# Every third weight subtract of the in-projection on GpSimd instead of VectorE

## The chip, the cores and the metric

The kernel runs on one core of a Trainium2 chip. The metric is the device time of one execution in microseconds; a profile of one execution, taken by the hardware profiler, comes with it. The engines are named as the profile names them: PE (TensorE, matmuls), PEld (its weight loads), DVE (VectorE), ACT (ScalarE), POOL (GpSimd) and SP (SyncE, which issues most DMAs).

## The reference

A two-layer streaming encoder on 256 tokens of width 1024, in float32. Each layer has a token mixer (retention and a convolution branch, both fed by one input projection), cross-attention into 256 memory tokens, and a gated MLP. The change touches the input projection `w_in`, 1024 x 10240 in each layer:

```python
def mixer_sublayer(u, cos, sin, w_in, ...):
    p = u @ w_in
    q, k, v, g_ret, c_in, gates = jnp.split(p, cuts, axis=-1)
    q = rotary(q, cos, sin) * (RET_QK_DIM ** -0.5)
    k = rotary(k, cos, sin)
    o = head_group_norm(chunk_retention(q, k, v), ret_gn_g)
    y_a = (jax.nn.silu(g_ret) * o) @ w_ret_out
    a, b = jnp.split(c_in, 2, axis=-1)
    c = causal_dwconv(a * jax.nn.sigmoid(b), conv_dw_w, conv_dw_b)   # 31 taps
    y_b = jax.nn.silu(layer_norm(c, conv_ln_g, conv_ln_b)) @ w_conv_out + b_conv_out
    g_a, g_b = jnp.split(jax.nn.sigmoid(gates + b_gate), 2, axis=-1)
    return (g_a * y_a + g_b * y_b) @ w_mix_out
```

## The kernel before

Every float32 matrix product is made of three products in the faster format `float32r`: each operand is split into a high half, the value rounded to that format, and a low half, what the rounding left (value minus high half). High times high, high times low and low times high are added up in PSUM.

**The weights.** All weights stream through SBUF. They are cut into chunks of 128 x 2048 (1 MB, one DMA issued by SP into one of four `raw` buffers) and each chunk into two units of 128 x 1024. `prepare` (L150) makes the halves of one unit: ScalarE copies `raw` to `whi` (L155), and VectorE subtracts, `wlo = raw - whi` (L156). There are four buffers of `whi` and four of `wlo` (`UNITS`), and `run` (L160) calls `prepare` until it is four units ahead of the steps whose matmuls have been issued. 420 units are prepared: in each layer 80 of `w_in` (78 in layer 0, whose first chunk is split elsewhere), 16 of `w_ret_out`, 16 of `w_xkv`, 8 each of four other matrices, 44 of `w_up` and 24 or 22 of the down projection.

**The in-projection** comes first in each layer: 8 chunks for the convolution branch (`in_b`, `in_a`), the first four on the not yet normalised input, then for each of four heads q and k (2 chunks), v and the gate g (4 chunks in all, through `token_step`), then 8 chunks for the merging gates. Between the matmuls of the heads stand the pieces of retention: `scores`, `attend`, whose normalisation takes a reciprocal root on GpSimd (L691, `rs`), which VectorE then multiplies by the mean (L693, `nmr`), and `gate`, where TensorE transposes the result (L703) and VectorE and ScalarE split it (L710, L711).

**The 31 taps of the convolution** are spread over the same steps as background work: most by ScalarE's product and VectorE's add (`tap`, L581 and L584), every third of half the channels by VectorE alone (`tap_alone`, L590), and 21 per layer by ScalarE into one of two buffers `moved` and an accumulating DMA issued by GpSimd (`tap_moved`, L599 and L602). In layer 0 VectorE also makes the rotary tables (L451 to L480) in the first 80 us.

**What sets the order.** The program is written step by step, and a scheduler with a model of time then sets the order of each engine's queue; each engine works through its own queue in that order and waits by semaphores. So an edit of one engine's work moves instructions of others.

Of the kernel before, what the change touches and what calls it, by code (L numbers as in the profile page):

```python
# [7 lines left out]
F32 = mybir.dt.float32  # L8
# [3 lines left out]
ALU = mybir.AluOpType  # L12
# [65 lines left out]
class Trunk:  # L78
    def __init__(self, ctx, tc, io):
        self.tc, self.nc, self.io = tc, tc.nc, io  # L80
        pool = lambda name, bufs, **kw: ctx.enter_context(tc.tile_pool(name=name, bufs=bufs, **kw))
        self.cp = pool("const", 1)
        self.wp = pool("weights", 3)
        self.bp = pool("blocks", 1)
        self.sp = pool("small", 2)
        self.pp = pool("psum", 1, space=bass.MemoryType.PSUM)
        self.steps = []
        self.uid = 0
        self.raws = {}
        self.streaming = False  # L90
        self.pin = None
        self.planned = 0
        self.background = []


    def nm(self, s):
# [53 lines left out]
    def prepare(self, src, at, kt, cols):  # L150
        nc, n = self.nc, kt * cols
        raw = self.fetch(src)[:, at:at + n]
        hi = self.wp.tile([P, 1024], F32R, name=self.nm("whi"), tag="whi", bufs=UNITS)
        lo = self.wp.tile([P, 1024], F32R, name=self.nm("wlo"), tag="wlo", bufs=UNITS)
        self.latest = nc.scalar.activation(hi[:, :n], raw, AF.Copy).ins  # L155
        nc.vector.tensor_tensor(lo[:, :n], raw, hi[:, :n].bitcast(F32), op=ALU.subtract)  # L156
        v = lambda t: t[:, :n].rearrange("p (k c) -> p k c", k=kt)
        return v(hi), v(lo)

# [1094 lines left out]
```

## Time and profile before

| | us |
|---|---|
| three runs: median (lowest to highest) | 1265.89 (1264.91 to 1268.05) |
| the profiled execution's own time | 1265.35 |
| its span, first to last instruction | 1263.5 |
| mean granted TensorE clock in it | 0.998 of full speed |
| L155 (copy to `whi`, ScalarE), 420 instructions | 439.5 |
| L156 (subtract to `wlo`, VectorE), 420 instructions | 508.0 |
| GpSimd's own work: L602 (issue of 42 DMAs), L691 (16 roots), L274 (9 roots) | 36.9, 17.0, 11.6 |

A row of a group names the line, the engine and the operation, what it writes and reads with the shape, the count, the busy time and the mean duration in ns of one; behind the second bar stands the idle time of the engine just before these instructions and what ended most of it. A row of a timeline begins with its start and its duration in us; where it ends with `x2` it is two instructions merged. A row of waits gives the total, the number of waits and the longest. Matmuls are pipelined: one begins before the one ahead of it has ended, and a busy TensorE is a TensorE that has something in its pipe.

### The profile page before, as it was taken

How to read it: one execution, taken by the hardware profiler on the slowest of the kernel's cores; microseconds unless marked ns; L12 is line 12 of the kernel's file. 1: busy time of each engine (PE TensorE's matmuls, PEld its weight loads, DVE VectorE, ACT ScalarE, POOL GpSimd, SP SyncE). 2: the span in 40 equal slices, each digit the busy share in tenths (PEclk: the TensorE clock that was granted, in tenths of full speed). 3: DMA queues.
4: the chain of work that ended last, by engine and by line, in shares of the span. 5: the costliest groups of instructions: out<-in, count | busy, mean ns of one | idle time of the engine just before them, and what ended most of it. 6: DMA issues, size and time to landing. Idle time of an engine off the chain costs nothing.

```text
span 1263.5 us, 18274 instructions
## 1 busy us (share of the span) xinstructions
PE 1251.2 (99%) x6914; PEld 1085.4 (86%) x6914; DVE 1010.9 (80%) x1540; ACT 858.8 (68%) x1428; POOL 66.8 (5%) x73
## 2 busy tenths in 40 slices
PE   9999999999999999999999999999999999999997
PEld 8988888888888898888898888888888888988886
DVE  7989988788787588886588899887887767888853
ACT  6798788867366456765458988788565565677642
POOL 0001111100000000000000111111000000000000
PEclk9999999999999999999999999999999999999999
DMA  8677787885554355554555877779754543455550
GB/s 311 213 237 218 216 234 217 244 282 179 195 172 162 113 194 199 195 192 161 205 190 186 252 210 219 228 209 278 270 179 160 195 159 142 171 212 198 177 192 34
DMA packets 40487, 252.66 MB, mean 200 GB/s; under 512 B 4688, under 2 KB 5968, under 8 KB 13520
## 3 DMA queue, kind: packets, MB, share of 16 engines
q1 hardware_dynamic: 34064, 228.96, 50.7%
q0 software_dynamic: 6048, 22.02, 9.1%
q8 instruction: 54, 0.88, 0.3%
q10 hardware_dynamic: 288, 0.52, 0.1%
q14 instruction: 33, 0.27, 0.1%
HBM read 228.42 MB, written 1.05 MB: 182 GB/s over the span
## 4 chain that ended last, share of the span: by engine, by line
PE 94%; DMA 2%; DVE 2%; ACT 1%; issue 1%; SPq 0%; POOL 0%; POOLq 0%; DVEq 0%
PE mm L239 32%; PE mm L214 28%; PE mm L212 14%; PE mm L1123 5%; PE mm L200 3%; PE mm L198 3%; PE mm L199 3%; PE mm L318 1%; PE mm L680 1%; DVE wlo L156 1%; DMA acc<-moved 1%; PE mm L926 1%; PE mm L928 1%; DMA raw<-in_mem_dram 1%; PE mm L927 1%
## 5 line engine op out<-in xcount | busy, mean ns | idle before, releaser
L155 ACT ACTIVATE whi<-raw 128x1024 fp32r<-128x1024 f32 (+1 forms) x420 | 439.5, 1053 | 297.0 <-PE mm L214 131.5
L156 DVE TENSOR_TENSOR wlo<-raw,whi 128x1024 fp32r<-128x1024 f32 (+1 forms) x420 | 508.0, 1214 | 134.2 <-ACT whi L155 120.4
L214 PE MATMUL mm<-blk,whi 128*128 128x512 f32 x1552 | 515.1, 395 | 0.0
L239 PE MATMUL mm<-whi,blk 128*128 128x512 f32 x1280 | 404.2, 392 | 0.0
L212 PE MATMUL mm<-blk,wlo 128*128 128x256 f32 x1552 | 391.5, 280 | 0.0
L214 PEld LDWEIGHTS mm<-blk,whi 128*128 128x128 f32 x1552 | 288.3, 188 | 63.2 <-DVE blk L190 0.7
L212 PEld LDWEIGHTS mm<-blk,wlo 128*128 128x128 f32 x1552 | 277.4, 189 | 5.3 <-DVE wlo L156 0.8
L239 PEld LDWEIGHTS mm<-whi,blk 128*128 128x128 f32 x1280 | 239.5, 188 | 48.7
L239 PE MATMUL mm<-wlo,blk 128*128 128x512 f32 x640 | 249.5, 391 | 0.0
L239 PEld LDWEIGHTS mm<-wlo,blk 128*128 128x128 f32 x640 | 120.3, 188 | 24.0
L581 ACT ACTIVATE prod<-blk,params 128x255 f32<-128x255 f32 (+20 forms) x224 | 94.1, 488 | 0.0
L200 PE MATMUL mm<-blk,wlo 128*128 128x256 f32 x288 | 81.4, 283 | 0.5 <-DVE wlo L156 0.5
L198 PE MATMUL mm<-blk,whi 128*128 128x256 f32 x288 | 81.8, 284 | 0.0
L199 PE MATMUL mm<-blk,whi 128*128 128x256 f32 x288 | 81.5, 283 | 0.0
L584 DVE TENSOR_TENSOR blk<-blk,prod 128x1020 f32<-128x1020 f32 (+21 forms) x56 | 65.5, 1170 | 8.2 <-ACT prod L581 7.7
L599 ACT ACTIVATE moved<-blk,params 128x227 f32<-128x227 f32 (+20 forms) x168 | 69.1, 482 | 0.0
L227 DVE TENSOR_TENSOR t<-mm,t 128x256 f32<-128x256 f32 x140 | 56.0, 415 | 2.3 <-ACT t L226 1.9
L200 PEld LDWEIGHTS mm<-blk,wlo 128*128 128x128 f32 x288 | 55.1, 191 | 0.6 <-DVE wlo L156 0.6
L198 PEld LDWEIGHTS mm<-blk,whi 128*128 128x128 f32 x288 | 55.1, 191 | 0.1
L199 PEld LDWEIGHTS mm<-blk,whi 128*128 128x128 f32 x288 | 55.1, 191 | 0.0
L602 POOL DMA_DIRECT2D acc<-moved x42 | 36.9, 878 | 342.0 <-ACT moved L599 206.5
L1123 PE MATMUL mm<-whi,blk 128*128 128x512 f32 x176 | 54.3, 389 | 0.0
(172 smaller groups left out, 1187.2 us busy)
## 6 DMA issues: line engine op xcount, KB each, us to landing
raw<-in_w_in_dram SPq DMA_DIRECT2D x79, 1024.0 KB, 4.8
raw<-in_w_up_dram SPq DMA_DIRECT2D x44, 1024.0 KB, 4.8
acc<-moved POOLq DMA_DIRECT2D x42, 512.0 KB, 5.4
raw<-in_w_ret_out_dram SPq DMA_DIRECT2D x16, 1024.0 KB, 6.6
raw<-in_w_xkv_dram SPq DMA_DIRECT2D x16, 1024.0 KB, 4.8
raw<-in_w_last_dram SPq DMA_DIRECT2D x11, 1024.0 KB, 4.8
raw<-in_w_conv_out_dram SPq DMA_DIRECT2D x8, 1024.0 KB, 4.8
raw<-in_w_mix_out_dram SPq DMA_DIRECT2D x8, 1024.0 KB, 4.8
```

The lines of the kernel that those rows point to most:

```text
L155: self.latest = nc.scalar.activation(hi[:, :n], raw, AF.Copy).ins
L156: nc.vector.tensor_tensor(lo[:, :n], raw, hi[:, :n].bitcast(F32), op=ALU.subtract)
L198: self.nc.tensor.matmul(out, wh[:, k, :], uh[:, k0 + k, :], start=a, stop=False)
L199: self.nc.tensor.matmul(out, wh[:, k, :], ul[:, k0 + k, :], start=False, stop=False)
L200: self.nc.tensor.matmul(out, wl[:, k, :], uh[:, k0 + k, :], start=False, stop=b)
L212: self.nc.tensor.matmul(ps[:, 0, :], w[1][:, k, :], u[0][:, k, :], start=False, stop=i == end)
L214: self.nc.tensor.matmul(ps, w[0][:, k, :], u.tile[:, k], start=i == 0, stop=False)
L239: mm = lambda a, b, p, q: self.nc.tensor.matmul(outs[t], a, b, start=p, stop=q)
L581: nc.scalar.activation(t[:, i, :m], X["c"][:, k, :m], AF.Copy, scale=self.par("conv_dw_w", L, k * TAPS + TAPS - 1 - s))
L584: nc.vector.tensor_tensor(cc, cc, t[:, :, :m], op=ALU.add)
L599: nc.scalar.activation(t[:, i, s:], X["c"][:, 4 + i, :N - s], AF.Copy, scale=self.par("conv_dw_w", L, (4 + i) * TAPS + TAPS - 1 - s))
L1123: mm = lambda x, y, p, e: self.nc.tensor.matmul(out, x, y[:, j, :], start=p, stop=e)
```

## The change

A counter of units is added to the class. Where a unit belongs to `w_in` and its number is a multiple of three, the same subtract is called on GpSimd in place of VectorE. Nothing else is edited; lines behind the edit are two higher.

```diff
@@ -90,7 +90,7 @@
         self.streaming = False
         self.pin = None
         self.planned = 0
-        self.background = []
+        self.background, self.count = [], 0
@@ -153,7 +153,9 @@
         hi = self.wp.tile([P, 1024], F32R, name=self.nm("whi"), tag="whi", bufs=UNITS)
         lo = self.wp.tile([P, 1024], F32R, name=self.nm("wlo"), tag="wlo", bufs=UNITS)
         self.latest = nc.scalar.activation(hi[:, :n], raw, AF.Copy).ins
-        nc.vector.tensor_tensor(lo[:, :n], raw, hi[:, :n].bitcast(F32), op=ALU.subtract)
+        self.count += 1
+        third = "w_in" in src.tensor.name and self.count % 3 == 0
+        (nc.gpsimd if third else nc.vector).tensor_tensor(lo[:, :n], raw, hi[:, :n].bitcast(F32), op=ALU.subtract)
```

The queues move at many places, since the scheduler plans anew. GpSimd's queue before, in layer 0 from the attention output of the second head to that of the third (`rs` are the reciprocal roots of the two halves of the tokens, `acc` the accumulating DMAs of the convolution):

```order
L602 DMA acc_178<-moved_27_177 128x1024
L691 TENSOR_TENSOR rs_1567<-ve_1565,mhalf 128x1
L602 DMA acc_178<-moved_26_176 128x1024
L691 TENSOR_TENSOR rs_1587<-ve_1585,mhalf 128x1
L602 DMA acc_178<-moved_27_177 128x1024
L602 DMA acc_178<-moved_26_176 128x1024
```

The same piece of GpSimd's queue in the changed kernel:

```order
L604 DMA acc_178<-moved_27_177 128x1024
L158 TENSOR_TENSOR wlo_1494<-raw_1487,whi_1493 128x1024
L693 TENSOR_TENSOR rs_1567<-ve_1565,mhalf 128x1
L604 DMA acc_178<-moved_26_176 128x1024
L158 TENSOR_TENSOR wlo_1654<-raw_1651,whi_1653 128x1024
L693 TENSOR_TENSOR rs_1587<-ve_1585,mhalf 128x1
L604 DMA acc_178<-moved_27_177 128x1024
L158 TENSOR_TENSOR wlo_1705<-raw_1698,whi_1704 128x1024
L604 DMA acc_178<-moved_26_176 128x1024
```

A subtract now stands ahead of each root and between the DMAs, and the second root waits behind `wlo_1654`. VectorE's queue before, at the same place (`nmr` needs the root of the same half; `t_242` and `t_249` are the outputs that TensorE transposes):

```order
L693 TENSOR_SCALAR nmr_1569<-mv_1563,rs_1567 128x1
L156 TENSOR_TENSOR wlo_1654<-raw_1651,whi_1653 128x1024
L658 TENSOR_TENSOR q_1536<-t_229_1537,t_230_1538 128x256
L659 TENSOR_TENSOR q_1536<-t_229_1537,t_230_1538 128x256
L689 TENSOR_SCALAR ve_1585<-mv_1583 128x1
L696 TENSOR_TENSOR t_242_1571<-t_242_1571,g_1473 128x512
L156 TENSOR_TENSOR wlo_1658<-raw_1651,whi_1657 128x1024
L693 TENSOR_SCALAR nmr_1589<-mv_1583,rs_1587 128x1
L584 TENSOR_TENSOR blk_175<-blk_175,prod_1687 128x4x245
```

And VectorE's queue there in the changed kernel:

```order
L695 TENSOR_SCALAR nmr_1569<-mv_1563,rs_1567 128x1
L660 TENSOR_TENSOR q_1536<-t_229_1537,t_230_1538 128x256
L661 TENSOR_TENSOR q_1536<-t_229_1537,t_230_1538 128x256
L691 TENSOR_SCALAR ve_1585<-mv_1583 128x1
L698 TENSOR_TENSOR t_242_1571<-t_242_1571,g_1473 128x512
L158 TENSOR_TENSOR wlo_1658<-raw_1651,whi_1657 128x1024
L695 TENSOR_SCALAR nmr_1589<-mv_1583,rs_1587 128x1
L586 TENSOR_TENSOR blk_175<-blk_175,prod_1687 128x4x245
```

Only `wlo_1654` is gone from it; what follows keeps its order. The beginning of GpSimd's streaming work in the changed kernel, where before the first root was followed by nothing until the DMAs of the convolution:

```order
L276 TENSOR_TENSOR rs_r_262<-rs_m_261,mhalf 128x2
L158 TENSOR_TENSOR wlo_152<-raw_111,whi_151 128x1024
L158 TENSOR_TENSOR wlo_301<-raw_294,whi_300 128x1024
L158 TENSOR_TENSOR wlo_472<-raw_469,whi_471 128x1024
L158 TENSOR_TENSOR wlo_551<-raw_544,whi_550 128x1024
```

Unit 3 (`wlo_152`), which VectorE subtracted right behind unit 2, now stands behind the first root, and units 6, 9 and 12 follow it. SP's queue is the same in both kernels.

## The prediction

> **What bounds the kernel now.** I read the page first: busy time, the chain that ended last, and the two groups that the change touches.
>
> ```profile
> span 1263.5 us, 18274 instructions
> PE 1251.2 (99%) x6914; PEld 1085.4 (86%) x6914; DVE 1010.9 (80%) x1540; ACT 858.8 (68%) x1428; POOL 66.8 (5%) x73
> PE 94%; DMA 2%; DVE 2%; ACT 1%; issue 1%; SPq 0%; POOL 0%; POOLq 0%; DVEq 0%
> L155 ACT ACTIVATE whi<-raw 128x1024 fp32r<-128x1024 f32 (+1 forms) x420 | 439.5, 1053 | 297.0 <-PE mm L214 131.5
> L156 DVE TENSOR_TENSOR wlo<-raw,whi 128x1024 fp32r<-128x1024 f32 (+1 forms) x420 | 508.0, 1214 | 134.2 <-ACT whi L155 120.4
> ```
>
> TensorE (PE) is busy for 99% of the span and makes 94% of the chain. GpSimd (POOL) is nearly unused. The subtract that is moved (L156) takes 1.21 us on VectorE (DVE), and VectorE has idle time in front of it, mostly waiting for ScalarE's copy. ScalarE (ACT) in its turn waits for TensorE to hand back a buffer: the weights are prepared as early as the four buffers let them be. Next I asked who TensorE ever waits for:
>
> ```profile
> PE nrm L405 <- DVE ones L391: 1.1, 1, 1.1
> PE mm L318 <- DVE blk L190: 0.7, 3, 0.3
> PE mm L680 <- ACT t L189: 0.6, 1, 0.6
> PE nrm L267 <- POOL rs_r L274: 0.5, 1, 0.5
> PE mm L200 <- DVE wlo L156: 0.5, 1, 0.5
> PE mm L318 <- ACT blk L189: 0.4, 1, 0.4
> PE nrm L259 <- DVE t L251: 0.3, 1, 0.3
> ```
>
> All waits together are 4.1 us, and one wait of 0.5 us is for a subtract. So **relieving VectorE can bring almost nothing**; the question is only whether the change makes something late enough for TensorE to notice. That is decided in the in-projection, so I took windows of it (columns: window, length, PE, PEld, DVE, ACT, POOL busy, clock, DMA share, GB/s): the early part, one period of a head in each layer, and the part of layer 1 up to its second head.
>
> ```profile
> 30.00:90.00 60.00, 60.00 (x420) 56.40 (x420) 56.53 (x82) 50.28 (x91) 1.91 (x2) 1.00 0.64 214
> 138.90:176.30 37.40, 37.40 (x186) 31.49 (x186) 33.48 (x56) 30.89 (x61) 5.69 (x6) 1.00 0.76 225
> 690.00:762.00 72.00, 71.39 (x361) 60.19 (x360) 63.77 (x95) 62.24 (x122) 7.91 (x9) 1.00 0.75 227
> 761.90:799.30 37.40, 37.40 (x187) 31.50 (x186) 33.51 (x56) 30.91 (x61) 5.69 (x6) 1.00 0.76 225
> ```
>
> The 80% of the whole is an average. Here VectorE works 33.5 of 37.4 us, and 56.5 of 60 in the early part. TensorE is at full clock and without a gap.
>
> **What is removed.** The in-projection's units, as the windows of L156 alone count them:
>
> ```profile
> 15.50:244.00 228.50, 94.18 (x78) 1.00 0.75 231
> 626.80:867.20 240.40, 96.95 (x80) 1.00 0.70 219
> ```
>
> They are 78 in layer 0 (the first chunk is prepared elsewhere) and 80 in layer 1, at places 1 to 78 and 211 to 290 of all 420; multiples of three are 26 and 26, so 52 subtracts leave VectorE. At 1.22 us that is 63 us of its busy time. Worth to TensorE: at most the 0.5 us above.
>
> **What is added.** 52 subtracts on GpSimd. No row shows one there; the nearest rows are GpSimd's own two-operand instruction on one or two elements, and VectorE's on this very tile.
>
> ```profile
> 298.38 0.70 POOL L274 TENSOR_TENSOR rs_r<-rs_m,mhalf 128x2 f32<-128x2 f32 x1 [24.30 <-DVE rs_m L273]
> 459.07 2.35 DVE L156 TENSOR_TENSOR wlo<-raw,whi 128x1024 fp32r<-128x1024 f32 x2
> 459.29 1.54 POOL L274 TENSOR_TENSOR rs_r<-rs_m,mhalf 128x2 f32<-128x2 f32 x1 [80.96 <-DVE rs_m L273]
> 138.94 1.17 DVE L584 TENSOR_TENSOR blk<-blk,prod 128x984 f32<-128x984 f32 x1
> 139.17 1.36 POOL L691 TENSOR_TENSOR rs<-ve,mhalf 128x1 f32<-128x1 f32 x1 [10.45 <-DVE ve L689]
> 176.35 1.15 DVE L584 TENSOR_TENSOR blk<-blk,prod 128x960 f32<-128x960 f32 x1
> 176.59 1.34 POOL L691 TENSOR_TENSOR rs<-ve,mhalf 128x1 f32<-128x1 f32 x1 [9.76 <-DVE ve L689]
> 213.23 1.12 DVE L584 TENSOR_TENSOR blk<-blk,prod 128x936 f32<-128x936 f32 x1
> 213.46 1.31 POOL L691 TENSOR_TENSOR rs<-ve,mhalf 128x1 f32<-128x1 f32 x1 [9.26 <-DVE ve L689]
> ```
>
> Duration: at least 1.22 us (I see no reason for GpSimd to be faster than VectorE), at most 0.70 + 2 x 1.22 = 3.14 us (its fixed cost, and the two operands read one after the other). I take 0.70 + 1.22 = **1.92 us**, nearest to both rows. [...]
>
> The same rows show the second cost. When VectorE is in a subtract or a convolution tap, that is in an instruction with two operands from SBUF, GpSimd's tiny instruction lasts 1.31 to 1.54 us in place of 0.70, and in the three pairs it shrinks by 0.02 and 0.03 us as the tap does (1.17, 1.15, 1.12): it **ends 0.42 or 0.43 us behind the tap's end** each time. GpSimd's read waits until VectorE's instruction is through. Whether VectorE waits likewise while GpSimd reads, the trace cannot show, since two elements are read in no time. [...]
>
> I take it that VectorE waits too: what makes GpSimd wait for a two-operand VectorE instruction is something that both need, and it would be as little free while GpSimd uses it. (Ends: no stop, and a stop for the whole duration.) So each moved unit takes 1.22 us off VectorE and stops it for up to 1.92 us. Not all of that stop counts: instructions with an operand from PSUM may run under it.
>
> ```profile
> L685 DVE BATCH_NORM_STATS2 bs<-mm 128x6 f32<-128x512 f32 x3 | 2.1, 692 | 0.9 <-PE mm L680 0.9
> L711 DVE SCALAR_TENSOR_TENSOR blk<-mm,params,blk 128x256 fp32r<-128x256 f32 x4 | 1.8, 476 | 0.7 <-ACT blk L710 0.7
> L227 DVE TENSOR_TENSOR t<-mm,t 128x256 f32<-128x256 f32 x4 | 1.6, 408 | 0.0
> L190 DVE TENSOR_TENSOR vlo<-mm,vhi 128x512 fp32r<-128x512 f32 x2 | 1.3, 680 | 0.0
> ```
>
> These are 6.8 of 33.5 us in the head's period, a fifth. VectorE takes its queue in order, so only those that stand at the front when GpSimd starts get through; I count half of the fifth, a tenth. The net addition to VectorE per moved unit is then 0.9 x 1.92 - 1.22 = **0.51 us** (by the ends: below nothing at 1.22, and 0.9 x 3.14 - 1.22 = 1.61 at 3.14).
>
> - Period of a head, 12 units, 4 moved: 33.48 + 2.0 = 35.5 of 37.4 us. VectorE still fits, with 1.9 us left where it had 3.9.
> - 690 to 762 us, 8 moved: 63.77 + 4.1 = 67.9 of 72. It fits.
> - 30 to 90 us, 7 moved: 56.53 + 3.6 = 60.1 of 60. **Full to the brim.**
>
> **What lies on TensorE's path.** A late VectorE costs nothing until its lateness passes what TensorE has in hand. For weights: a unit lasts TensorE 37.4 / 12 = 3.1 us and three other buffers are full, so 9.3 us less 1.05 us for the copy and 1.22 us for the subtract, some 7 us. For the attention output, the place on GpSimd's queue where a reciprocal root now stands behind a subtract:
>
> ```profile
> 143.29 0.68 DVE L696 TENSOR_TENSOR t<-t,g 128x512 f32<-128x512 f32 x1
> 148.83 0.60 PE L703 MATMUL mm<-ident,t 128*128 128x128 f32 x4
> ```
>
> The product ends at 143.97 and TensorE transposes it at 148.83: 4.9 us in hand. The new queue adds up to one subtract (1.92 us) in front of `rs_1587`; VectorE's `nmr` waits for it, and behind `nmr` the taps. That fits into 4.9 us. The accumulating DMAs on the same queue (GpSimd issues 42) start up to 1.92 us later; each frees one of two buffers, so only a delay of a whole turn would reach ScalarE. SP's queue is as before. The early part has less in hand:
>
> ```profile
> 18.28 1.61 POOL L274 TENSOR_TENSOR rs_r<-rs_m,mhalf 128x2 f32<-128x2 f32 x1 [17.83 <-DVE rs_m L273]
> 22.98 0.28 PE L200 MATMUL mm<-blk,wlo 128*128 128x256 f32 x1
> 22.40 2.83 DVE L371 SCALAR_TENSOR_TENSOR t<-h,params,nrm 128x256 f32<-128x256 f32 x7 [0.48 <-ACT rstd L361]
> 44.87 1.22 DVE L584 TENSOR_TENSOR blk<-blk,prod 128x1020 f32<-128x1020 f32 x1 [0.87 <-ACT prod L581]
> ```
>
> Unit 3 now stands behind the root that ends at 19.89: 19.89 + 1.92 = 21.81, and up to 1.22 later if a VectorE subtract is in the way, while TensorE reads it at 22.98. That costs nothing to 0.05 us. From 22.40 to the 0.87 us before 44.87 VectorE has next to no idle time, and in it makes the normalised input that TensorE needs; unit 6's stop makes that later by 1.92 - 1.22 = 0.7 us.
>
> **The sum**, against the profiled execution's own 1265.35 us (its span of 1263.5 and 1.85 around it; the median of the three runs is 0.5 higher): the normalised input 0.7; the full stretch to 90 us, 1.0 (0.1 over, and the 3.5 us of idle in it, some of which are waits for inputs that cannot be filled: from nothing to 3.5, taken near the bottom as there are buffers behind it); then 154 us of layer 0 (90 to 244) and 240 us of layer 1 (627 to 867), 394 / 37.4 = 10.5 periods at 0.3 us (ends: nothing, if all stays within the 4.9 and 7 us; 2.0, if none of the added time is filled into idle time; near the bottom for the same reason) = 3.2. Together 4.9, so **1270 us**. At a duration of 1.22 us it would be 1265.4; at 3.14 VectorE lacks 7.8 us before 90 us and 2.5 us in each period: 1265.35 + 0.7 + 7.8 + 26 = 1300.
>
> **The rivals.**
> - *VectorE is not stopped.* GpSimd's reads only wait, or slip in beside VectorE's. Then VectorE sheds 1.22 us per unit, nothing becomes late, and TensorE is where it was: 1265. For it: only one direction of the wait is seen, and the 7 and 4.9 us in hand. It decides at a stop of 1.22 / 0.9 = 1.36 us per subtract: below that VectorE gains.
> - *The subtract takes GpSimd much longer*, 2.8 to 3.14 us: VectorE's period is then 33.48 + 4 x (0.9 x 2.8 - 1.22) = 38.7 of 37.4 us and TensorE follows VectorE: 1265.35 + 10.5 x 1.3 + 7 = 1286, up to 1300. For it: nothing shows GpSimd on so many elements. Against it: nothing shows its fixed cost to grow with size.
> - *Faster*: VectorE's relief removes TensorE's waits. At most 4.1 us of waits exist, most of them in lines of the start (L405, L318, L259): 1261 to 1264.
> - *The change does not do what it says*: excluded, the built order has 52 subtracts on POOL.
>
> **How the numbers follow.** Forecast (stopped, just fitting), 1266 to 1278: 0.52. Not stopped, 1264 to 1267: 0.30. Long subtract, 1278 to 1300: 0.14. Faster: 0.04. A measurement of this kernel tells 0.3%, 3.8 us, from no change. Slower by more: the long case and 0.41 of the forecast's 0.52, so 0.55; faster 0.04; within it 0.41. The range leaves out the faster case's most and the long case's upper part: 1263.5 to 1288.
>
> **What would show it.** GpSimd's subtract at 1.9 us or more, longer where VectorE is in a tap; VectorE's two-operand instructions stretched, or idle with GpSimd as the releaser, in the in-projection alone; new TensorE waits for `wlo`, `blk` (L190) or the transposed product, first before 90 us; everything behind 867 us (layer 1) shifted and not stretched. VectorE's instructions unstretched beside a long GpSimd subtract would refute the stop; a TensorE span unchanged with stretched VectorE would mean that I mis-sized the idle time that can be filled.

## The result, and the profile after

| | before | changed |
|---|---|---|
| median (lowest to highest), us | 1265.89 (1264.91 to 1271.25) | 1281.32 (1280.53 to 1283.02) |
| runs | 5 | 5 |
| the profiled execution | 1265.35 | 1281.31 |
| its span | 1263.5 | 1279.5 |

The changed kernel takes 1.0117 times as long (95% interval 1.0097 to 1.0137), 15.4 us more by the medians. The forecast of 1270 had the direction, and the range of 1263.5 to 1288 holds the time, but the band of the forecast's own case, 1266 to 1278, does not; the loss is three times the 4.9 us of the sum.

The page of the changed kernel, its busy times, its chain and the groups that the change touches:

```profile
span 1279.5 us, 18348 instructions
PE 1255.9 (98%) x6914; PEld 1084.4 (85%) x6914; DVE 1028.9 (80%) x1488; ACT 856.9 (67%) x1428; POOL 218.1 (17%) x125
PE 76%; DVE 13%; ACT 4%; issue 3%; DMA 2%; POOL 1%; SPq 0%; POOLq 0%; DVEq 0%; ACTq 0%
L158 DVE TENSOR_TENSOR wlo<-raw,whi 128x1024 fp32r<-128x1024 f32 (+1 forms) x368 | 469.9, 1281 | 121.9 <-ACT whi L155 107.8
L158 POOL TENSOR_TENSOR wlo<-raw,whi 128x1024 fp32r<-128x1024 f32 x52 | 152.9, 2947 | 306.0 <-PE mm L214 172.4
L586 DVE TENSOR_TENSOR blk<-blk,prod 128x1020 f32<-128x1020 f32 (+21 forms) x56 | 79.0, 1410 | 16.7 <-ACT prod L583 16.4
```

52 subtracts have left VectorE, and still it is busy for 18.0 us more than before. Its remaining subtracts have gone from a mean of 1214 to 1281 ns, and the 56 taps on the last line are longer too. VectorE is now 13% of the chain, where it was 2%. The line of GpSimd's subtract by itself (least, median and greatest duration in ns, then first and last start):

```profile
L158 POOL TENSOR_TENSOR wlo<-raw,whi x52: 2375/2488/6389, 19.7 to 874.4; 128x1024 fp32r<-128x1024 f32 x52
```

Undisturbed it takes 2.4 us, twice VectorE's 1.2, but some last up to 6.4. TensorE's waits (total, number, longest), which were 4.1 us in all before, are now 13.9:

```profile
PE mm L202 <- DVE wlo L158: 3.1, 4, 1.2
PE mm L241 <- POOL wlo L158: 2.5, 3, 1.4
PE mm L241 <- DVE wlo L158: 1.5, 2, 1.1
...
PE mm L667 <- DVE k L660: 1.2, 1, 1.2
PE mm L202 <- POOL wlo L158: 0.8, 1, 0.8
PE mm L705 <- DVE nmr L695: 0.8, 1, 0.8
```

TensorE waits for low halves from both engines, and for rotated keys (`k`). These rows have grown by 9.8 us; TensorE's busy time has grown too, by 4.7 us for the same 6914 matmuls (1251.2 to 1255.9). Where matmuls come apart without an idle gap between them, no wait is listed. To see where, I paired TensorE's 6914 matmuls of both traces in order and took how much later each begins (my own working from the start times, 30 neighbours averaged at each point):

| time in before, us | 20 | 45 | 90 | 140 | 177 | 245 | 300 | 645 | 762 | 867 | 1250 |
|---|---|---|---|---|---|---|---|---|---|---|---|
| later in the changed kernel, us | 0.7 | 3.3 | 5.7 | 6.2 | 8.4 | 11.8 | 13.5 | 13.6 | 14.7 | 14.7 | 14.8 |

So 5.7 us go before 90 us, 6.1 from there to 245 us, where layer 0's in-projection ends, 1.8 behind it, and 1.2 in all of layer 1, although both layers move 26 subtracts. The 1.8 arise between 280 and 300 us: VectorE has waited 2.4 us for the last accumulating DMA there, and TensorE then waits 1.5 us for two low halves. (Experiment 1 below loses 1.2 us at this place without any subtract on GpSimd, so the subtracts need not be the cause.) The last 1.2 us of the span's 16.0 arise behind the last matmul; where an expectation below speaks of about 3 us in layer 1, they seem to be counted in. The windows of the changed kernel that hold the same matmuls as the three of the prediction (30 to 90 us, one head of layer 0, the same head of layer 1) show the two layers apart (columns as there):

```profile
31.80:95.70 63.90, 61.32 (x421) 56.71 (x421) 59.08 (x73) 49.88 (x91) 24.29 (x10) 1.00 0.59 191
145.10:184.70 39.60, 38.43 (x186) 31.16 (x186) 38.56 (x52) 31.04 (x62) 18.92 (x10) 1.00 0.73 217
776.60:814.00 37.40, 37.40 (x186) 31.50 (x185) 32.83 (x55) 30.71 (x60) 18.15 (x10) 1.00 0.83 232
```

The head in layer 0 has grown from 37.40 to 39.60 us and VectorE in it from 33.48 to 38.56: VectorE is full and TensorE follows it. The same head in layer 1 is as long as before, and VectorE has *gained* 0.7 us. Four subtracts are moved in each. The first window is 3.9 us longer, with VectorE 2.5 us busier.

VectorE and GpSimd in the layer 0 head, from the timeline (start, duration, and in brackets the idle time before):

```profile
149.23 3.74 DVE L659 TENSOR_TENSOR t<-t,sin 128x512 f32<-128x512 f32 x1
149.74 2.67 POOL L158 TENSOR_TENSOR wlo<-raw,whi 128x1024 fp32r<-128x1024 f32 x1
...
161.25 3.95 POOL L158 TENSOR_TENSOR wlo<-raw,whi 128x1024 fp32r<-128x1024 f32 x1 [1.94 <-issue]
162.99 2.50 DVE L660 TENSOR_TENSOR k<-t,t 128x256 f32<-128x256 f32 x1
165.26 0.51 PE L241 MATMUL mm<-wlo,blk 128*128 128x512 f32 x1 [0.62 <-POOL wlo L158]
...
779.39 0.68 DVE L659 TENSOR_TENSOR t<-t,sin 128x512 f32<-128x512 f32 x1
781.32 0.41 DVE L660 TENSOR_TENSOR q<-t,t 128x256 f32<-128x256 f32 x1
```

VectorE's L659 takes 0.68 us and L660 0.41 where no subtract runs beside them (the last two rows); here 3.74 and 2.50. The wait goes both ways: GpSimd's second subtract needs 3.95 us, since it started behind VectorE's work, and once it reads, VectorE's next instruction stands until GpSimd has ended at 165.20. Then TensorE waits for that unit.

Two more places show what the prediction had no term for. The first, at 92 us:

```profile
91.43 1.21 DVE L158 TENSOR_TENSOR wlo<-raw,whi 128x1024 fp32r<-128x1024 f32 x1
91.85 6.39 POOL L158 TENSOR_TENSOR wlo<-raw,whi 128x1024 fp32r<-128x1024 f32 x1 [1.98 <-issue]
92.57 1.19 DVE L586 TENSOR_TENSOR blk<-blk,prod 128x1000 f32<-128x1000 f32 x1
...
94.81 1.18 DVE L586 TENSOR_TENSOR blk<-blk,prod 128x996 f32<-128x996 f32 x1
96.72 2.60 DVE L158 TENSOR_TENSOR wlo<-raw,whi 128x1024 fp32r<-128x1024 f32 x1 [0.72 <-ACT whi L155]
```

By the profile GpSimd's subtract starts at 91.85, but four two-operand instructions of VectorE (the third, a subtract, left out here) run on, back to back and at their usual length. Only where VectorE has a gap (0.72 us ahead of 96.72) does GpSimd get on; it ends at 98.24, 2.25 us after the tap ahead of the gap, and meanwhile stops VectorE's next subtract, which takes 2.60. So GpSimd is starved by a dense VectorE, and its unit is ready 4 us late. The second, at 249 us:

```profile
248.96 0.86 POOL L604 DMA_DIRECT2D acc<-moved  x1 [9.29 <-DMA acc<-moved]
249.26 6.39 DVE L158 TENSOR_TENSOR wlo<-raw,whi 128x1024 fp32r<-128x1024 f32 x1
249.52 5.03 POOL L158 TENSOR_TENSOR wlo<-raw,whi 128x1024 fp32r<-128x1024 f32 x2
252.27 0.50 PE L241 MATMUL mm<-wlo,blk 128*128 128x512 f32 x1 [1.43 <-POOL wlo L158]
```

GpSimd's queue stood 9.29 us for the accumulating DMA before to land; two subtracts had piled up behind it and ran one after the other; VectorE was stopped through both (6.39 us for a subtract of 1.2), and TensorE waited 1.43 us.

### The profile page after: what moved, and what is told of

Same layout as the page of the kernel before. It is cut to its first block, busy times and chain, and to the rows that moved or that the text cites. A ratio compares the mean times of both kernels' runs of the same rounds, so it can differ in the third digit from the quotient of the medians.

```text
span 1279.5 us, 18348 instructions
## 1 busy us (share of the span) xinstructions
PE 1255.9 (98%) x6914; PEld 1084.4 (85%) x6914; DVE 1028.9 (80%) x1488; ACT 856.9 (67%) x1428; POOL 218.1 (17%) x125
## 4 chain that ended last, share of the span: by engine, by line
PE 76%; DVE 13%; ACT 4%; issue 3%; DMA 2%; POOL 1%; SPq 0%; POOLq 0%; DVEq 0%; ACTq 0%
PE mm L216 26%; PE mm L241 22%; PE mm L214 13%; PE mm L1125 4%; DVE wlo L158 4%; ACT whi L155 2%; PE mm L202 1%; PE mm L200 1%; PE mm L201 1%; PE mm L320 1%; DVE blk L586 1%; ACT prod L583 1%; DMA acc<-moved 1%; DVE t L659 1%; PE mm L682 1%
## 5 line engine op out<-in xcount | busy, mean ns | idle before, releaser
L158 DVE TENSOR_TENSOR wlo<-raw,whi 128x1024 fp32r<-128x1024 f32 (+1 forms) x368 | 469.9, 1281 | 121.9 <-ACT whi L155 107.8
L241 PE MATMUL mm<-whi,blk 128*128 128x512 f32 x1280 | 404.4, 392 | 0.0
L216 PEld LDWEIGHTS mm<-blk,whi 128*128 128x128 f32 x1552 | 288.3, 188 | 63.1 <-DVE blk L192 0.7
L158 POOL TENSOR_TENSOR wlo<-raw,whi 128x1024 fp32r<-128x1024 f32 x52 | 152.9, 2947 | 306.0 <-PE mm L214 172.4
L583 ACT ACTIVATE prod<-blk,params 128x255 f32<-128x255 f32 (+21 forms) x224 | 94.6, 493 | 0.0
L586 DVE TENSOR_TENSOR blk<-blk,prod 128x1020 f32<-128x1020 f32 (+21 forms) x56 | 79.0, 1410 | 16.7 <-ACT prod L583 16.4
L276 POOL TENSOR_TENSOR rs_r<-rs_m,mhalf 128x2 f32<-128x2 f32 x9 | 11.1, 1238 | 411.6 <-DVE rs_m L275 405.8
L201 PEld LDWEIGHTS mm<-blk,whi 128*128 128x128 f32 x288 | 55.1, 191 | 0.0
```

The lines of the kernel that those rows point to most:

```text
L158: (nc.gpsimd if third else nc.vector).tensor_tensor(lo[:, :n], raw, hi[:, :n].bitcast(F32), op=ALU.subtract)
L201: self.nc.tensor.matmul(out, wh[:, k, :], ul[:, k0 + k, :], start=False, stop=False)
L216: self.nc.tensor.matmul(ps, w[0][:, k, :], u.tile[:, k], start=i == 0, stop=False)
L241: mm = lambda a, b, p, q: self.nc.tensor.matmul(outs[t], a, b, start=p, stop=q)
L583: nc.scalar.activation(t[:, i, :m], X["c"][:, k, :m], AF.Copy, scale=self.par("conv_dw_w", L, k * TAPS + TAPS - 1 - s))
L586: nc.vector.tensor_tensor(cc, cc, t[:, :, :m], op=ALU.add)
```

## The experiments

Theory: GpSimd's *read* takes something that VectorE's instructions need, and VectorE, made late by it, makes TensorE late. Rivals: the new order of the queues, the units that GpSimd itself delivers late, the write, and the mere use of GpSimd. The expectations speak of time by which VectorE is "stretched": the sum, over its instructions, of what each lasted beyond the median of its form in the profile before. That is my working from the trace; in the changed kernel it is 77.0 us, 48.6 in layer 0 and 28.4 in layer 1. The page's busy time is an independent measure of it. All edits are to the changed kernel.

**1. Nothing subtracted for the moved units.**

```diff
-        (nc.gpsimd if third else nc.vector).tensor_tensor(lo[:, :n], raw, ...)
+        if third:
+            lo = hi
+        else:
+            nc.vector.tensor_tensor(lo[:, :n], raw, ...)
```

> The 52 units have no subtract at all: TensorE is given the high half in place of the low one (this part of the product is left out), so VectorE is relieved of 52 subtracts and GpSimd gets nothing. Theory LOCK (reads of GpSimd and two-operand instructions of VectorE exclude each other, and that is what costs): 1262 to 1266 us, as before. Theory ORDER (the new order of the queues costs, not GpSimd's work): 1272 us or more, since the scheduler plans anew here as well. If relief of VectorE is worth something, this shows how much at the most: below 1262.

1266.34 us, ratio 1.0002 (0.9988 to 1.0015). Its busy times:

```profile
PE 1251.2 (99%) x6914; PEld 1085.3 (86%) x6914; DVE 957.7 (76%) x1488; ACT 859.1 (68%) x1428; POOL 64.8 (5%) x73
```

VectorE is relieved of 1010.9 - 957.7 = 53.2 us and TensorE gains nothing. So the new plan of the scheduler, as it is without these subtracts, costs nothing, and the relief is worth nothing: taking the subtracts off VectorE altogether leaves the time where it was. Against this run VectorE is busy for 1028.9 - 957.7 = 71.2 us more in the changed kernel: that is what GpSimd's 52 reads cost it, 1.37 us each.

**2. GpSimd subtracts, TensorE does not wait for it.**

```diff
+        if third:
+            nc.gpsimd.tensor_tensor(lo[:, :n], raw, hi[:, :n].bitcast(F32), op=ALU.subtract)
+            lo = hi
```

The `else` with VectorE's subtract stands as in 1; here and in 3 and 4 it is left out of the diff.

> GpSimd makes the 52 subtracts as in the change, but TensorE takes the high half for these units (this part of the product is left out) and no engine but the buffers' next user waits for GpSimd's result. Theory LOCK through VectorE (VectorE is stopped 1.56 us per subtract and everything else comes late): nearly all of the 15.4 us stays, 1276 us or more, and VectorE's busy time is near 1029 us. Theory LATE UNIT (the time is lost where TensorE waits for a unit that GpSimd finishes late): 1266 to 1270 us although VectorE's instructions are stretched as much. Both in part: in between.

1278.29 us, ratio 1.0095 (1.0078 to 1.0112); VectorE busy 1025.0. TensorE's longest waits:

```profile
PE mm L206 <- DVE wlo L162: 4.3, 4, 1.7
PE mm L245 <- DVE wlo L162: 2.6, 3, 1.4
```

With no matmul that reads GpSimd's result, 12.4 of the 15.4 us remain: most of the loss comes through VectorE. What the late units add, 3.0 us by the medians, agrees with the 3.3 us that TensorE waited for them in the changed kernel, but the intervals of the two ratios overlap. Nor are the two runs alike in clock: in this one's profile the granted clock was 0.5 for 3.4 us, from 61.6 us on, behind the wait of 1.7 us, and in the changed kernel's it was not. An estimate of what this took is half of 3.4 us, 1.7 us; VectorE's part may thus be nearer to 11 us and that of the late units nearer to 5. A late GpSimd could also hold back the loads into `raw`, which it reads, but ScalarE waited for `raw` of `w_in` only 0.6 us here, and 0.5 us in the kernel before.

**3. GpSimd only writes.**

```diff
+        if third:
+            nc.gpsimd.memset(lo[:, :n].bitcast(F32), 0.0)
```

> On GpSimd a memset of the same 128 x 1024 low half takes the place of the subtract (the low half of these units is left out), and TensorE waits for it: GpSimd writes as much but reads nothing. Theory LOCK: no VectorE instruction with two operands in SBUF is stretched, VectorE's busy time is about 1011 - 63 = 948 us, and the time is 1262 to 1267 us. If writing collides as well, VectorE is stretched and the time is 1272 us or more. Theory ORDER: 1272 us or more with nothing stretched.

1264.95 us, ratio 0.9994 (0.9985 to 1.0003). Busy times:

```profile
PE 1251.0 (99%) x6914; PEld 1085.2 (86%) x6914; DVE 957.6 (76%) x1488; ACT 858.8 (68%) x1428; POOL 114.0 (9%) x125
```

VectorE is as little busy as without any of it, to 0.1 us. No instruction of VectorE lasts over 0.1 us beyond its usual time. Writing the same tile on GpSimd, and waiting for GpSimd, are free here, though a memset takes 1.0 us and the subtract 2.4; the reads are what collides. This run also settles the order of the queues: by the order of their starts and the names of what they write and read, 1471 of VectorE's 1488 instructions stand in the same sequence as in the changed kernel, and the time is that of the kernel before.

**4. GpSimd reads one operand.**

```diff
+        if third:
+            nc.gpsimd.tensor_copy(lo[:, :n], raw)
```

> GpSimd copies raw to the low half in place of the subtract (the low half of these units is wrong by that): one operand is read in place of two, TensorE waits for it as in the change. Theory LOCK FOR THE READING TIME: the copy takes 1.0 to 1.5 us and VectorE's stops fall to half, 30 to 45 us in all, less than the 63 us it sheds: 1264 to 1269 us. Theory LOCK FOR THE UNIT'S WAIT (any read has to wait for a gap in VectorE's queue, and the unit comes late by that): 1271 us or more.

1267.38 us, ratio 1.0014 (1.0005 to 1.0024). Busy times, and GpSimd's group:

```profile
PE 1251.2 (99%) x6914; PEld 1084.9 (86%) x6914; DVE 982.8 (78%) x1488; ACT 858.3 (68%) x1428; POOL 139.6 (11%) x125
L159 POOL CAST wlo<-raw 128x1024 fp32r<-128x1024 f32 x52 | 77.8, 1496 | 341.3 <-PE mm L217 213.0
```

VectorE loses 982.8 - 957.7 = 25.1 us, 0.48 per copy: the stop is there, with one operand instead of two it is a third of the 1.37, and that fits into what TensorE has in hand. The loss of time does not go in proportion: 71.2 us of stops cost 15.4, 25.1 us cost 1.7 (against the median of 1265.64 that the kernel before had beside this run).

**5. The subtract in four pieces of 256 columns**, so that VectorE might get in between them.

```diff
+        parts = [slice(i, i + 256) for i in range(0, n, 256)] if third else [slice(0, n)]
+        for s in parts:
+            (nc.gpsimd if third else nc.vector).tensor_tensor(lo[:, s], raw[:, s], ...)
```

> GpSimd makes each of the 52 subtracts in four instructions of 256 columns. Theory SUM OF STOPS (the time lost goes with VectorE's stopped time less the subtracts it sheds): the reads are as long in all, so VectorE is stretched by 65 to 90 us in all and the loss stays at 8 to 20 us. Theory SINGLE STOP (a stop of 2 us at a bad place is what hurts): each stop is near 0.6 us, VectorE gets in between, and the loss falls to under 5 us. GpSimd's wait for a gap comes four times per unit, so the unit itself may take 5 us and more from first to last piece.

1287.34 us, ratio 1.0163 (1.0145 to 1.0182): both expectations missed. GpSimd's group, TensorE's two longest waits, and VectorE's for the accumulated taps:

```profile
L160 POOL TENSOR_TENSOR wlo<-raw,whi 128x256 fp32r<-128x256 f32 x208 | 216.0, 1084 | 274.3 <-PE mm L216 172.4
...
PE nrm L271 <- POOL rs_r L278: 6.5, 1, 6.5
PE mm L243 <- POOL wlo L160: 4.7, 4, 1.9
...
DVE blk L615 <- DMA acc<-moved: 10.5, 2, 9.8
```

VectorE is relieved, to 1000.9 us of busy time, below the kernel before. But GpSimd needs 216 us instead of 153, and its units and the accumulating DMAs that it issues come later. By the paired matmuls 6 us are lost by 45 us, where TensorE waits 2.9 us for one unit of GpSimd's, and 8.5 us between 250 and 280. There the last DMA of layer 0 lands so late that VectorE stands for 9.8 us, and `rs_m`, the root and TensorE behind it. (The kernel before has such a wait as well, of 4.0 us, and the memset kernel one of 5.2, without harm.) Why the DMA took longer to land here I did not trace. A less busy VectorE is thus no cure by itself.

**6. Layer 1 alone** (`and self.count > 200`).

> Only layer 1's 26 units go to GpSimd. In the change the shift of TensorE's matmuls grows by 13.5 us in layer 0 and by about 3 us in layer 1, where VectorE's stretched time is 28 us against 30 us that it sheds. If the layers add up: 1267 to 1270 us. If layer 1 got away lightly only because layer 0 had set other instructions' times: 1273 us or more.

1266.53 us, ratio 1.0015 (0.9997 to 1.0032): not told from no change, though VectorE's busy time is 1008.3, that is 26 subtracts lighter and as many stops heavier. Two of the ten executions took 1272.54 and 1274.76 us; what these lost was not traced.

**7. From unit 28 on** (`and self.count > 27`): the first nine moved units stay on VectorE.

> Layer 0's first nine multiples of three, up to unit 27, stay on VectorE; the other 43 go to GpSimd. In the change 5.4 us are lost up to that place, where VectorE was busy for 56.5 of 60 us before. If that part is lost because VectorE is full there: 1274 to 1277 us. If what is lost there only comes earlier than it would otherwise (a later wait takes it): 1279 us or more.

1273.36 us, ratio 1.0059 (1.0042 to 1.0076). This is just below the first band and clear of the second. So the first nine units, subtracted by 98 us, cost 8.0 us of the 15.4, and the other 17 of layer 0 most of the rest: by the paired matmuls 5.5 us between 90 and 245. The window of the layer 0 head, and TensorE's wait in it at the place that is shown above for the changed kernel:

```profile
139.30:178.70 39.40, 38.22 (x187) 31.15 (x186) 38.41 (x52) 30.90 (x61) 18.93 (x10) 1.00 0.74 217
...
159.33 0.50 PE L241 MATMUL mm<-wlo,blk 128*128 128x512 f32 x1 [0.66 <-POOL wlo L158]
```

The head is as long as in the change and the same wait stands in it, although this kernel came into the head only 0.4 us late. What is lost there is made there.

**8. Another third** (`self.count % 3 == 1`): why does layer 0 lose and layer 1 not? A head has 12 units, so multiples of three fall at the same places in each head of a layer; but layer 0 counts 78 units and layer 1 begins at 211, so the places differ between the layers. With this third, layer 0 gets the places that layer 1 has in the change.

> The units with remainder 1 by three go to GpSimd instead of those with remainder 0: 26 in layer 0 and 27 in layer 1, at other places among the heads' chunks. If the loss goes with VectorE's total of stopped time, it is as large as in the change, 1278 to 1285 us, again most of it in layer 0, whose VectorE has more to do. If it goes with the place of the units (which instruction of VectorE stands next to them, which DMA stands ahead of them), the loss differs, and layer 1, which in the change lost 3 us and in this one gets other places, may lose as much as layer 0 did (13 us).

1276.03 us, ratio 1.0077 (1.0062 to 1.0092), below what was expected for the total, and little of it lost in the heads of either layer: by the paired matmuls 4.8 us are lost by 22 us, 2.6 more by 140, nothing between 140 and 245, and 4.3 behind 867 us. The first and the last of these losses each start with a single wait, in turn the second and the first row:

```profile
PE mm L241 <- ACT whi L155: 2.4, 1, 2.4
PE nrm L261 <- DVE t L253: 2.3, 1, 2.3
```

**9. The other third from unit 28 on** (`self.count % 3 == 1 and self.count > 27`).

> Units 28, 31, 34 ... of layer 0's in-projection and the matching ones of layer 1 (number 1 more than a multiple of three) on GpSimd, the first nine of layer 0 left on VectorE. PLACE IN THE HEAD (what a stopped VectorE costs depends on which of a head's twelve weight units GpSimd takes, because each stands at another distance from the work that TensorE waits for next): the heads of layer 0 lose 0 to 2 us, where the run from unit 28 with multiples of three lost 7.3; layer 1 as in the first run of this third, 0 to 3; together 1265.5 to 1270. STATE OF THE EARLY PART (that run's heads lost nothing because it had already been late before 90 us, so that the buffers were in another state): the heads lose 5 to 8 us as with the multiples of three, 1271 to 1277. VectorE's instructions stretched by 50 to 62 us in both.

1266.21 us, ratio 1.001 (1.0001 to 1.0019): PLACE IN THE HEAD. The layer 0 head's window:

```profile
140.50:177.80 37.30, 37.30 (x186) 31.43 (x185) 32.55 (x52) 30.63 (x60) 17.96 (x10) 1.00 0.82 232
```

As many subtracts as in 7, but of the units 28, 31, 34 instead of 30, 33, 36, and from 90 to 245 us 0.3 us are lost instead of 5.5: the head has 32.55 us of VectorE where 7 has 38.41. The 17 subtracts of layer 0 stretch VectorE's instructions by 14.9 us here and by 31.9 in 7. (In both layers together it is 47.4 us, a little under the expected 50 to 62.) The profiled execution was by chance the longest of 11, at 1273.15 us; by the paired matmuls its excess lies between 245 and 280 us, where VectorE waited 6.3 us for the last accumulating DMA and TensorE 3.4 us for the root behind it.

**10. The remaining third** (`self.count % 3 == 2`): layer 1 now has the places that layer 0 has in the change.

> Units 2, 5, 8 ... (number 2 more than a multiple of three). Counted from each layer's own first unit of the in-projection, layer 1 then has the places that layer 0 has in the change, and layer 0 a third set not yet seen. PLACE IN THE HEAD: layer 1 loses 5 to 8 us between 690 and 870 us, where the change lost 1; layer 0 not told by it. LAYER (layer 0 loses because of what it alone has, the rotary tables before 80 us and what they leave late): layer 1 loses 0 to 2 us again, and layer 0 the most. Total by either 1272 to 1285, VectorE stretched by 60 to 80 us.

1280.08 us, ratio 1.012 (1.0106 to 1.0134). Layer 1 now loses 6.0 us between 762 and 867 us. Its head's window, and the same place once more:

```profile
768.40:807.90 39.50, 38.36 (x187) 31.16 (x186) 38.51 (x52) 30.99 (x61) 18.92 (x10) 1.00 0.75 215
...
784.51 3.96 POOL L158 TENSOR_TENSOR wlo<-raw,whi 128x1024 fp32r<-128x1024 f32 x1 [1.95 <-issue]
786.25 2.50 DVE L660 TENSOR_TENSOR k<-t,t 128x256 f32<-128x256 f32 x1
788.53 0.51 PE L241 MATMUL mm<-wlo,blk 128*128 128x512 f32 x1 [0.63 <-POOL wlo L158]
```

The stall of layer 0 appears in layer 1, alike within hundredths of a microsecond. (Behind 867 us this run loses 5.5 more, where VectorE waits 6.4 us for the last accumulating DMA.) In layer 0 this third loses 4.4 us before 90 us and nothing from there to 245. So it is the place among the head's units that decides, and not the layer; nor is earlier lateness needed. It can add to the loss, though: the third that lost 0.3 us in experiment 9 lost 2.6 by 140 us in 8, where the first nine units were moved too.

## Why the prediction was right in direction and short in size

- **The range** holds the time only because it took in the lower part of the long case. The forecast's own case ended at 1278, 3 us too early, so that the time lies inside is in part luck.
- **TensorE bounds, and relieving VectorE is worth nothing:** shown by experiments 1 and 3. The relief itself was put at 63 us and is 53.2. A subtract's record overlaps its neighbour's (91.43 + 1.21 is 92.64, the next starts at 92.57): VectorE's durations add up to 59.9 us less in experiment 1 (1104.5 to 1044.6), and 6.7 us of this were overlap, which busy time does not count twice.
- **The lock, both ways:** right in the main. VectorE's instructions with two operands from SBUF stand while GpSimd reads (1.37 us per subtract, 0.48 per copy of experiment 4), and not while it only writes (none over 0.1 us in experiment 3). That those with an operand from PSUM run on is right too: 46 of them overlap one of the 52 subtracts, and none lasts over 0.1 us longer than usual. But a few instructions with a single operand from SBUF are stopped as well, in the making of the rotary tables: the copy in the first row below takes 2.48 us in place of 0.29, beside a subtract that GpSimd makes from 19.69 to 22.94 us. Nor does the order of the starts alone tell which of the two stands, if the profile's start times hold: three of VectorE's instructions that started after GpSimd's subtract at 91.85 us (at 92.57, 93.68 and 94.81) went ahead of it at their usual 1.2 us.
- **The duration:** 1.92 us was taken, 2.40 is the undisturbed time and 2.95 the mean. Yet this isn't what failed: the stop per subtract was put at 0.9 x 1.92 = 1.73 us and measured at 1.37, the net addition to VectorE at 0.51 and measured at 18.0 / 52 = 0.35.
- **The step that failed** is the term of the sum for the time that TensorE feels, "10.5 periods at 0.3 us" and "the full stretch to 90 us, 1.0", each "near the bottom". I spread the addition evenly over the periods. It is not even: by place, four subtracts stop VectorE for 9.1 us in the head of layer 0 (beyond the usual durations: 3.06 at L659 and 2.09 at L660 above, 2.20 and 1.78 in the second and third rows below) and for 2.9 in that of layer 1 (1.77, 0.24 and 0.86 in the next three, and nothing for the last subtract). So 35.5 of 37.4 us became 38.56 of 39.60 in layer 0 and 32.83 of 37.40 in layer 1. Layer 0's 154 us, 4.1 periods, were given 1.2 us and lost 6.1 (1.5 a period, nearer to the upper end of 2.0 that I had named than to 0.3); layer 1's 6.4 periods were given 1.9 and lost 1.2; the part to 90 us was given 1.7 and lost 5.7. For the 1.8 us between 280 and 300 us and the 1.2 behind the last matmul the sum had no term.

Rows of the timeline of the changed kernel for these stops:

```profile
20.61 2.48 DVE L455 CAST kept<-blk 128x256 fp32r<-128x256 f32 x1
...
170.00 3.37 DVE L586 TENSOR_TENSOR blk<-blk,prod 128x972 f32<-128x972 f32 x1
180.43 3.00 DVE L158 TENSOR_TENSOR wlo<-raw,whi 128x1024 fp32r<-128x1024 f32 x1 [0.35 <-ACT whi L155]
...
783.62 2.95 DVE L586 TENSOR_TENSOR blk<-blk,prod 128x980 f32<-128x980 f32 x1 [0.21 <-ACT prod L583]
795.54 1.46 DVE L158 TENSOR_TENSOR wlo<-raw,whi 128x1024 fp32r<-128x1024 f32 x1
801.51 2.02 DVE L586 TENSOR_TENSOR blk<-blk,prod 128x968 f32<-128x968 f32 x1 [0.81 <-ACT prod L583]
```

- **"In hand, some 7 us" for weights** assumed that GpSimd's subtract starts when its copy is done. It did not: it is starved by a dense VectorE (6.39 us at 91.85), or queued behind a DMA issue that waits for the one before to land (9.29 us at 248.96). I had asked how late the subtracts make the DMAs, and not how late the waiting DMAs make the subtracts. TensorE's 3.3 us of waits for GpSimd's units are this.
- **The root behind a subtract:** about right; one wait of 0.8 us for `nmr` in the whole run.
- **Layer 1 behind 867 us shifted and not stretched, the first waits before 90 us:** both seen.
- **Rivals.** *Not stopped* is refuted. (The 1.36 us at which it was to be decided, 1.22 / 0.9, is a duration and not a stop. The measured stop of 1.37 us is to be held against what leaves VectorE, put at 1.22 us and measured at 53.2 / 52 = 1.02.) *Long subtract* named the mean duration (2.8 to 3.14 us) and its band of 1278 to 1300 holds the time, but by a VectorE too slow in every period, and in layer 1 it gained. With hindsight that case deserved more than 0.14, since its price in layer 0 came true.

What stays open: why an accumulating DMA sometimes lands late enough to reach TensorE (experiments 5, 9 and 10), why the time behind the last matmul grew, and how the first nine units' 8.0 us split between VectorE's full queue and GpSimd's late units.

## What to carry to other kernels

Moving an operation to an idle engine is not free when that engine's reads stop the busy one, as they did here (71.2 us of VectorE by 52 subtracts); price the stop at up to the whole duration of the slower copy (here 2.3 us of 2.4 per subtract in the head of layer 0, 0.7 in that of layer 1), and see whether the busy engine is working or waiting at each place where it falls. An average over periods hides this: 17 moved units of layer 0 cost 5.5 us or 0.3 between 90 and 245 us, depending on which units of a head were taken (experiments 7 and 9). And before anything is queued on the idle engine, ask what already waits in its queue, and what the relief could bring at best: by experiment 1 it could bring nothing here.

## What the runs showed of the hardware beside this

Behind some of TensorE's longer waits the granted clock dropped. Windows around and behind the longest wait (3.5 us) of experiment 10 (PEclk is the third figure from the end):

```profile
913.00:917.00 4.00, 1.30 (x5) 1.09 (x6) 4.00 (x5) 1.06 (x1) 0.00 (x0) 0.96 0.33 84
917.00:921.00 4.00, 4.00 (x12) 3.13 (x12) 4.00 (x6) 1.06 (x1) 0.00 (x0) 0.61 0.72 252
921.00:925.00 4.00, 4.00 (x20) 3.29 (x19) 2.59 (x4) 1.06 (x1) 0.00 (x0) 1.00 0.90 356
```

TensorE was busy for a third of the first window; in the next it passed 12 matmuls, in the one after 20. The same followed the wait of 3.4 us in experiment 9 (0.50 from 278 to 282 us), those of 2.9 and 6.5 us in experiment 5 (0.50 from 38 to 41 us, 0.53 from 290 to 294) and those of 2.3 and 2.4 us in experiment 8 (0.50 from 21 to 25 us, 0.70 from 901 to 905), so a part of what these runs lost is the clock. Shorter waits did so at some times and not at others: in experiment 2 the clock fell to 0.66 (63 to 66 us) behind a wait of 1.7 us, and stayed at 1.00 (227 to 231 us) behind one of 1.9. So some of these waits cost more than themselves: an estimate for experiment 10, from a clock of 0.61 over 4 us, is 1.6 us beyond its 3.5. In the changed kernel the longest is 1.4 us, behind which the clock stayed at 1.00 (252 to 258 us), and its windows above stand at 1.00.
